# A diffusion layer with expert retrieval: last heads of two blocks ahead of the late projections, PSUM banks used twice, and modulation rows by a transpose and DRAM

## Chip, cores and metric

One core of one Trainium2 chip runs the whole program. TensorE (PE) does the matmuls, VectorE (DVE), ScalarE (ACT) and GpSimd (POOL) the rest, SyncE (SP) issues most of the DMAs. The metric is the device time of one execution in microseconds; less is better. The kernel before took 1765.1 us (median of 3 runs, 1762.88 to 1768.2).

## The reference

One layer on 512 latent tokens of 1024 features (with 256 context tokens that only the scans read), all in float32. What matters of it:

```
m = silu(c) @ w_ada + b_ada                       # 6 * 1024 values
sh1, sc1, g1, sh2, sc2, g2 = split(m, 6)
u   = (layer_norm(x) * (1 + sc1) + sh1) @ w_in
mix = two_way_scans(u)                            # 8 heads of 128, RMS norm and gates
x   = layer_norm(ALPHA * x + g1 * (mix @ w_out), ln_gamma[0], ln_beta[0])
h   = layer_norm(x) * (1 + sc2) + sh2
y   = peer(h)        # queries, top 16 of 128 x 128 keys, 8 heads, gathered experts
x   = layer_norm(ALPHA * x + g2 * y, ln_gamma[1], ln_beta[1])
```

The four rows g1, sh2, sc2 and g2 have 1024 values each, one for each feature, and are wanted on all 128 partitions, since tokens lie on partitions.

## The kernel before

The program goes through the stages scans (`mixer`, to about 434 us), output projection with its norms (`out_proj_early` and `out_proj`, to about 496 us), retrieval (`Peer.run`, to about 1724 us) and a tail with the last norm (`finish`). A scheduler sets the order of instructions on each engine by priorities and data, except in stretches that are marked as ordered by hand; ACT in the tail is one (its order is that of the code).

**Modulation.** `mods_second` multiplies 24 columns of 128 weights with silu(c) on DVE (`column`, L215) and gathers the sums as columns of the tile `m2` [128, 32]: columns 0 to 7 are g1, 8 to 15 sh2, 16 to 23 sc2, 24 to 31 g2 (those by `mods_last` during the retrieval). To turn eight columns into a row on all partitions, `mod_half` (L259) lets PE multiply each column, broadcast to 128 x 128, with the identity, four to a bank of 512 (`prow`, L265; the trace counts two instructions for each), and ACT copies the bank (L267). g1 is then multiplied into w_out on DVE (L232), half by half. `mod_row` (L269) does both halves of a row, for sc2 at the end of `out_proj_early`, sh2 in `out_proj`, and g2 in the tail.

**Output projection.** Tokens form four blocks of 128. Seven of eight heads are ready early: blocks 0 and 1 (`NB` = 2) are projected during the scans and kept as `parts` together with ALPHA times x (L662). When the last head is there (`lasth`, `lastl`: high and low part of float32 in the fast matmul type, so each product is three matmuls, L139 to L141), the loop over b (L719 to L755) does for each block: a matmul with the identity that brings `parts` into PSUM (b < 2, L725), the last head's three matmuls for each half, statistics on DVE (L727), the norm's affine steps (`affine`, L134 and L135) into x1, a second norm and its affine into h2 with sc2 and sh2, eight transposes on PE (`pht`, L749) and the split into hh (ACT, L751) and hl (DVE, L752). Blocks 2 and 3 are projected inside the loop by `late_block` (L704), after block 0 and after block 1: ALPHA x by a matmul (L709, tile `xe`), then 42 matmuls of seven heads. Accumulators are the banks `po` (blocks 0 and 1, one after the other), `pl2` (block 2) and `pl3` (block 3), two banks each; `pht` has the other two. After the last head of block 3 come the first queries of blocks 0 and 1 (`first_queries(0)`, 48 matmuls, into `po`) and their scores (`pss`, L764), which share the loop's end with the norm of block 3; `first_queries(2)` closes the stage.

**Tail.** `rows` (a tile `Gn`) holds g2, ln_gamma and ln_beta. `finish` (L1187) is called for block 3 (its y is `yg` in SBUF) and blocks 0 to 2: y times g2 (L1195), plus ALPHA x1 (L1196), statistics (L1197), affine (L134, L135) and a write to the output (L1201). PE still combines y of blocks 0 to 2 while this runs.

Of the kernel before, what the change touches and what calls it, by code (L numbers as in the profile page):

```python
# [19 lines left out]
D = 1024  # L20
# [11 lines left out]
class Net:  # L32
# [155 lines left out]
    def mods_second(self, pers, pool):  # L188

        nc, a = self.nc, self.a
        H = D // 2
        mm = pool.tile([128, 24, 2], F32, name="m2h")
        self.m2 = pers.tile([128, 32], F32, name="m2")
        self.b2 = pers.tile([128, 32], F32, name="b2col")
        nc.sync.dma_start(self.b2, a["b2col"])
        nc.vector.tensor_scalar(self.b2[:, 16:24], self.b2[:, 16:24], 1.0, None, op0=OP.add)
        gain = pool.tile([128, 2], F32, name="gain")
        nc.sync.dma_start(gain, a["gains"])  # L200
        sr = pool.tile([128, 2, H], F32, name="silrow")
        for h in range(2):
            cr, t1 = (pool.tile([128, H], F32, name="wada2", bufs=3) for _ in range(2))
            nc.sync.dma_start(cr, a["crow"][:, h * H:(h + 1) * H].to_broadcast([128, H]))
            self.log_sigmoid(sr[:, h], cr, t1, t1)
            nc.scalar.activation(sr[:, h], sr[:, h], AF.Exp)
            nc.vector.tensor_tensor(sr[:, h], sr[:, h], cr, op=OP.mult)
        nc.sync.dma_start(self.sild, sr[0:1].rearrange("p h k -> p (h k)"))
        yield True

        def column(j):
            for h in range(2):
                w = pool.tile([128, H], F32, name="wada2", bufs=3)
                nc.sync.dma_start(w, a["w_ada2"][j, h])
                nc.vector.scalar_tensor_tensor(w, w, 1.0, sr[:, h], op0=OP.mult, op1=OP.mult,  # L215
                                               accum_out=mm[:, j, h:h + 1])

        def close(js):
            nc.vector.tensor_tensor(self.m2[:, js], mm[:, js, 0], mm[:, js, 1], op=OP.add)
            nc.vector.tensor_tensor(self.m2[:, js], self.m2[:, js], self.b2[:, js], op=OP.add)  # L220
        for j in range(8):
            column(j)
            if j % 2:
                yield True
        close(slice(0, 8))
        for hf in range(2):
            g1 = pool.tile([128, H], F32, name="g1")
            self.mod_half(g1, self.pj, 0, hf, "pj")
            for k in range(8):
                raw = pool.tile([128, H], F32, name="wada2", bufs=3)  # L230
                nc.sync.dma_start(raw, a["w_out"][k * 128:(k + 1) * 128, hf * H:(hf + 1) * H])
                nc.vector.scalar_tensor_tensor(raw, raw, gain[:, k // 4:k // 4 + 1], g1, op0=OP.mult, op1=OP.mult)  # L232
                hi = pool.tile([128, H], F32R, name="wosh")
                nc.scalar.activation(hi, raw, AF.Copy)
                nc.vector.tensor_tensor(raw.bitcast(F32R), raw, hi, op=OP.subtract)
                for i, t in enumerate((hi.bitcast(F32), raw)):
                    nc.sync.dma_start(self.wod[hf, i, :, k, :], t)
                yield True
                if k % 2:
                    j = 8 + hf * 8 + k - 1  # L240
                    column(j)
                    column(j + 1)
                    yield True
        close(slice(8, 24))

    def mods_last(self, pool):

# [8 lines left out]
            yield  # L256
        nc.vector.tensor_tensor(m2, m2, self.b2[:, 24:32], op=OP.add)

    def mod_half(self, out, ps, i, hf, ptag):  # L259

        nc = self.nc
        p = ps.tile([128, 512], F32, name="prow", tag=ptag)
        for k in range(4):
            j = i * 8 + hf * 4 + k
            nc.tensor.matmul(p[:, k * 128:(k + 1) * 128], self.m2[:, j:j + 1].to_broadcast([128, 128]),  # L265
                             self.ident, start=True, stop=True)
        nc.scalar.activation(out, p, AF.Copy)  # L267

    def mod_row(self, pool, ps, i, name, ptag):  # L269
        r = pool.tile([128, D], F32, name=name)  # L270
        for hf in range(2):
            self.mod_half(r[:, hf * 512:(hf + 1) * 512], ps, i, hf, ptag)
        return r


    def first_norm(self, pool, ps, xt, b):
# [361 lines left out]
    def out_proj_early(self, last, ps):  # L638
# [11 lines left out]
        for b in range(NB):  # L650
# [8 lines left out]
            for hf in range(2):  # L659
# [1 line left out]
                x, p = (t.rearrange("p (k c) -> p k c", k=4) for t in (xs[hf], ps_[hf]))  # L661
                nc.vector.scalar_tensor_tensor(r, x, ALPHA, p, op0=OP.mult, op1=OP.add)  # L662
                self.parts[b, hf] = r
        self.sc2 = self.mod_row(wo, ps, 2, "sc2", "pj2")

    def out_proj(self, pool, mpool, pers, ps, last):
        nc, a = self.nc, self.a
# [17 lines left out]
        nc.sync.dma_start(bet, a["ln_b"][0:1].to_broadcast([128, D]))  # L685
        self.sk = pers.tile([128, 2, 128], F32, name="sk")
        nc.sync.dma_start(self.sk, a["skT"])
        sh2 = self.mod_row(pool, ps, 1, "sh2", "pht")
        slabs, self.q0 = [], []
        for i in range(2):  # L690
            qh, ql = (mpool.tile([128, 8, 128], F32R, name=f"{n}{i}") for n in ("wq0h", "wq0l"))
# [6 lines left out]
        nc.vector.tensor_scalar(aid, self.ident, ALPHA, None, op0=OP.mult)  # L698

        banks = lambda n: [ps.tile([128, 512], F32, name=f"{n}{hf}", bufs=1) for hf in range(2)]  # L700
        r3, r0, r2 = (banks(n) for n in ("pl3", "po", "pl2"))
        rl = {0: r0, 2: r2, 3: r3}

        def late_block(b):  # L704
            sl = slice(b * 128, (b + 1) * 128)
# [4 lines left out]
            for g in self.groups:  # L710
                self.project_heads(rl[b], g, self.split_heads(g, sl), False, False)

        def first_queries(b0):
            cs = slice(b0 * 128, (b0 + 2) * 128)
            for (qh, ql), p, q in zip(slabs, banks("po"), self.q0):
                for k in range(8):
                    self.mm3(p[:, cs], qh[:, k, :], ql[:, k, :], self.hh[:, k, cs], self.hl[:, k, cs], k == 0, k == 7)
                nc.scalar.activation(q[:, cs], p[:, cs], AF.Copy)
        for b in range(4):  # L719
            sl = slice(b * 128, (b + 1) * 128)  # L720
            st = pool.tile([128, 2, 6], F32, name="sto", bufs=2)
            r = rl[b] if b in rl else banks("po")
            for hf, (wh, wl) in enumerate(self.w):
                if b < NB:
                    nc.tensor.matmul(r[hf], self.ident, self.parts[b, hf], start=True, stop=False)  # L725
                self.mm3(r[hf], lh[:, sl], ll[:, sl], wh[:, last, :], wl[:, last, :], False, True)
                nc.vector.bn_stats(st[:, hf, :], r[hf])  # L727
            if b == 3:
                first_queries(0)
                self.yg = pers.tile([128, D], F32, name="yg")  # L730
                self.S0 = self.yg.rearrange("p (b s n) -> p b s n", b=4, s=2)
                self.scores(self.q0, ps, "pht", [((0, 2), lambda s: self.S0[:, 0:2, s, :])])
            x1 = x1s[b] if b < 2 else pool.tile([128, D], F32, name="x1", bufs=2)
            stats = self.norm_scale(pool, st, "o")
            for hf, p in enumerate(r):
                cs = slice(hf * 512, (hf + 1) * 512)
                self.affine(x1[:, cs], p, stats, gam[:, cs], bet[:, cs])
            nc.scalar.dma_start(self.x1d[b], x1)
            h2 = (h2s[b] if b < 2 else pers.tile([128, D], F32, name="h2_3") if b == 3 else
                  pool.tile([128, D], F32, name="h2", bufs=2))  # L740
            stats = self.norm_stats(pool, x1, "p")
            for cs in (slice(0, 512), slice(512, D)) if b == 3 else (slice(0, D),):
                self.affine(h2[:, cs], x1[:, cs], stats, sc2[:, cs], sh2[:, cs])
            self.h2[b] = h2
            for g in range(2):
                p = ps.tile([128, 4, 128], F32, name="pht")
                for k in range(4):
                    kk = g * 4 + k
                    nc.tensor.transpose(p[:, k, :], h2[:, kk * 128:(kk + 1) * 128], self.ident)  # L749
                hi, lo = self.hh[:, g * 4:g * 4 + 4, sl], self.hl[:, g * 4:g * 4 + 4, sl]  # L750
                nc.scalar.activation(hi, p, AF.Copy)  # L751
                nc.vector.tensor_tensor(lo, p, hi, op=OP.subtract)  # L752
            if b < NB:
                late_block(b + NB)
        first_queries(2)  # L755

    def scores(self, qT, ps, tag, dst):

# [143 lines left out]
class Peer:  # L902
# [300 lines left out]
    def run(self, es, out):  # L1203
# [14 lines left out]
        with ExitStack() as e0:  # L1218
# [78 lines left out]
            with ExitStack() as e1:  # L1297
# [38 lines left out]

                rows = w.tile([128, NG, self.GN, self.GT], F32, name="Gn", bufs=2)
                rows = rows.rearrange("p g n t -> p (g n t)").rearrange("p (i d) -> p i d", i=3)
                for hf in range(2):
                    n.mod_half(rows[:, 0, hf * 512:(hf + 1) * 512], hps, 3, hf, "pH")  # L1340
                nc.sync.dma_start(rows[:, 1], a["ln_g"][1:2].to_broadcast([128, D]))
                nc.sync.dma_start(rows[:, 2], a["ln_b"][1:2].to_broadcast([128, D]))
                nc.scalar.preload_act_table_set("natural_log_exp_and_others")
# [9 lines left out]
def build(tc, a, out):  # L1353
    with ExitStack() as es:
        n = Net(tc, a)
        n.h2 = {}
        n.consts(es)
        dp = es.enter_context(tc.tile_pool(name="x1d", bufs=1, space=bass.MemoryType.DRAM))
        n.x1d = dp.tile([4, 128, D], F32, name="x1d")
        n.wod = dp.tile([2, 2, 128, 8, 512], F32, name="wod")  # L1360
        n.sild = dp.tile([1, D], F32, name="sild")
        n.mixer(es)
        Peer(n).run(es, out)

# [16 lines left out]
```

## Time and profile before

| what | us or share |
|---|---|
| median of 3 runs (lowest, highest) | 1765.1 (1762.88, 1768.2) |
| the profiled execution's own time | 1758.76 |
| its span | 1756.6 |
| PE busy | 1699.8, 97% |
| weight loads (PEld) | 1486.9, 85% |
| DVE busy | 1447.2, 82% |
| ACT busy | 833.2, 47% |
| POOL busy | 406.7, 23% |

The span is what the trace shows between the first and the last instruction; 2.2 us of the execution lie around it. All rows below are from this one execution. A row of a timeline is a group of instructions that follow each other; its bracket says how long the engine stood idle before it and what ended that. Matmuls overlap, so that the start of the next row says more than the length of the last.

### The profile page before, as it was taken

Reading aid. Unit: us, or ns where it says so; the run is one execution under the profiler, and the core shown is the slowest. Engines: PE = TensorE matmul, PEld = TensorE weight load, DVE = VectorE, ACT = ScalarE, POOL = GpSimd, SP = SyncE. Lnnn points to the kernel's source line nnn. Section 1 sums busy time; section 2 is a strip of 40 time slices with the busy share of each in tenths; the row PEclk is TensorE's granted clock in tenths of the full one; section 3 lists DMA queues with packets and bytes.
Section 4 is the critical chain, followed back from the end, with each engine's and each line's share of the span. In section 5 each row is a group of like instructions: output and inputs, shape, how many; then the busy total and the mean of one; then the engine's idle time right before and its main releaser. Section 6 shows DMA issues by size and latency. Waiting matters only on the chain. (4 is left out here: it accounts for less than half of the span.)

```text
span 1756.6 us, 28197 instructions
## 1 busy us (share of the span) xinstructions
PE 1699.8 (97%) x10501; PEld 1486.9 (85%) x10501; DVE 1447.2 (82%) x2917; ACT 833.2 (47%) x1417; POOL 406.7 (23%) x286
## 2 busy tenths in 40 slices
PE   6999999989999999999999999999999999999997
PEld 3888877877778999999998999999999998888886
DVE  6688988877779999999996878777777786776768
ACT  4677677655133355676674333333333333333332
POOL 0000000000023102238422544443444342111000
PEclk8999999999989999999999999999999999999999
DMA  8444435242322257989999999989999989999862
GB/s 321 122 127 162 139 96 182 95 179 101 108 73 85 73 152 290 332 298 322 332 333 355 368 341 351 323 304 334 325 309 338 321 299 309 351 332 305 270 217 96
DMA packets 174811, 428.99 MB, mean 244 GB/s; under 512 B 14993, under 2 KB 78801, under 8 KB 170578
## 3 DMA queue, kind: packets, MB, share of 16 engines
q1 hardware_dynamic: 137234, 290.87, 48.5%
q0 software_dynamic: 36864, 134.23, 21.8%
q8 instruction: 82, 1.34, 0.3%
q10 hardware_dynamic: 576, 2.10, 0.3%
q14 instruction: 55, 0.45, 0.1%
HBM read 378.38 MB, written 48.76 MB: 243 GB/s over the span
## 5 line engine op out<-in xcount | busy, mean ns | idle before, releaser
L139 PE MATMUL pH<-hh,uh 128*128 128x384 f32 x1024 | 350.3, 342 | 1.1 <-ACT gels L1111 1.1
L141 PE MATMUL pH<-hh,ul 128*128 128x384 f32 x1024 | 347.7, 340 | 1.5 <-DVE ul L1098 1.5
L140 PE MATMUL pH<-hl,uh 128*128 128x384 f32 x1024 | 347.0, 339 | 0.0
L139 PE MATMUL y<-vh,ah 128*128 128x512 f32 x768 | 302.8, 395 | 2.9 <-ACT ah L1137 2.9
L140 PE MATMUL y<-vl,ah 128*128 128x512 f32 x768 | 301.5, 393 | 0.1
L141 PE MATMUL y<-vh,al 128*128 128x512 f32 x768 | 301.5, 394 | 0.0
L1098 DVE TENSOR_TENSOR vl<-vr,vh 128x1024 fp32r<-128x1024 f32 x128 | 156.7, 1224 | 151.7 <-ACT vh L1096 150.7
L1167 POOL DMA_INDIRECT erow<-in_u_dram,ix x128 | 187.8, 1467 | 370.4 <-DVE scr L1176 219.1
L1167 POOL DMA_INDIRECT erow<-in_v_dram,ix x128 | 185.4, 1448 | 327.3 <-DVE yg L1184 179.8
L1096 ACT ACTIVATE vh<-vr 128x1024 fp32r<-128x1024 f32 x128 | 135.1, 1057 | 195.2 <-issue 125.9
L1137 ACT ACTIVATE ah<-gel 128x384 fp32r<-128x384 f32 x128 | 66.8, 524 | 276.6 <-DVE gel L1134 273.6
L139 PEld LDWEIGHTS pH<-hh,uh 128*128 128x128 f32 x1024 | 192.4, 188 | 3.8 <-ACT gels L1111 1.4
L140 PEld LDWEIGHTS pH<-hl,uh 128*128 128x128 f32 x1024 | 192.8, 188 | 2.7
L141 PEld LDWEIGHTS pH<-hh,ul 128*128 128x128 f32 x1024 | 192.4, 188 | 2.6 <-DVE ul L1098 2.4
L1096 ACT ACTIVATE uh<-ur 128x1024 fp32r<-128x1024 f32 x128 | 135.0, 1056 | 121.2 <-PE pH L140 75.3
L141 PEld LDWEIGHTS y<-vh,al 128*128 128x128 f32 x768 | 144.9, 189 | 33.6
L139 PEld LDWEIGHTS y<-vh,ah 128*128 128x128 f32 x768 | 144.7, 188 | 33.0 <-ACT ah L1137 3.4
L140 PEld LDWEIGHTS y<-vl,ah 128*128 128x128 f32 x768 | 144.9, 189 | 30.6 <-DVE vl L1098 0.5
L1098 DVE TENSOR_TENSOR ul<-ur,uh 128x1024 fp32r<-128x1024 f32 x128 | 155.6, 1216 | 16.0 <-PE pH L141 13.9
L1184 DVE SCALAR_TENSOR_TENSOR yg<-erow,act,yg 128x1024 f32<-128x1024 f32 x127 | 162.2, 1277 | 0.1
L1176 DVE SCALAR_TENSOR_TENSOR scr<-erow,h 128x1024 bf16<-128x1024 f32 x128 | 155.8, 1218 | 0.0
L139 PE MATMUL pc<-hTh,wh 128*128 128x512 f32 (+1 forms) x304 | 109.5, 360 | 0.9 <-ACT V L407 0.7
(367 smaller groups left out, 3047.0 us busy)
## 6 DMA issues: line engine op xcount, KB each, us to landing
ur<-in_uT_dram SPq DMA_DIRECT2D x128, 512.0 KB
vr<-in_v_dram SPq DMA_DIRECT2D x128, 512.0 KB
Gd<-stage SPq DMA_DIRECT2D x24, 1024.0 KB
Gn<-Gd SPq DMA_DIRECT2D x16, 1536.0 KB
wraw<-in_w_cf_dram SPq DMA_DIRECT2D x24, 512.0 KB
wada<-in_w_ada_dram SPq DMA_DIRECT2D x48, 256.0 KB
Hd<-gels SPq DMA_DIRECT2D x56, 192.0 KB
gel<-Hd SPq DMA_DIRECT2D x56, 192.0 KB
```

The lines of the kernel that those rows point to most:

```text
L139: mm(out, lh, rh, start=start, stop=False)
L140: mm(out, lh, rl, start=False, stop=False)
L141: mm(out, ll, rh, start=False, stop=stop)
L1096: nc.scalar.activation(hi, raw, AF.Copy)
L1098: sub = eng.tensor_tensor(lo, raw, hi, op=OP.subtract)
L1137: nc.scalar.activation(ah, g, AF.Copy)
L1167: nc.gpsimd.indirect_dma_start(out=e, out_offset=None, in_=a[src], in_offset=bass.IndirectOffsetOnAxis(ap=self.ix[:, j:j + 1], axis=0))
L1176: nc.vector.scalar_tensor_tensor(scr, e, 1.0, h2, op0=OP.mult, op1=OP.mult, accum_out=dots[:, j:j + 1])
L1184: nc.vector.scalar_tensor_tensor(y, e, act[:, j:j + 1], y, op0=OP.mult, op1=OP.add)
```

## The change

**Rows.** `mod_half` goes. `to_rows` takes n columns of `m2` (8 or 16), transposes them with one PE instruction into [n, 128], copies that with ACT and writes it to a DRAM tile `m2d` from GpSimd's queue. The new `mod_row` reads a row back from `m2d` to all partitions, from GpSimd's queue too. g1 is written as a row once and read in two halves, sh2 and sc2 are written together at the end of `mods_second`, g2 in the tail. The columns 8 and 9 of `mods_second` move ahead of the work on w_out.

**Order.** The loop's body becomes two functions, `last_head(b)` and `norms(b)`, and the calls are written out. The banks are `po`, `pl1` and `pl2` for blocks 0, 1 and 2, and `po` once more for block 3; the first queries go into `pl1` (blocks 0 and 1) and `pl2` (blocks 2 and 3).

```diff
-            self.mod_half(g1, self.pj, 0, hf, "pj")
+            self.mod_row(g1, 0, slice(hf * H, (hf + 1) * H))
...
+    def to_rows(self, js, pool, ps, tag):
+
+        nc, n = self.nc, js.stop - js.start
+        p = ps.tile([n, 128], F32, name="prow", tag=tag)
+        nc.tensor.transpose(p, self.m2[:, js], self.ident)
+        r = pool.tile([24, 128], F32, name="mrows")[0:n]
+        nc.scalar.activation(r, p, AF.Copy)
+        nc.gpsimd.dma_start(self.m2d[0, js, :], r)
+
+    def mod_row(self, out, i, cs=slice(0, D)):
+
+        row = self.m2d[:, i * 8:(i + 1) * 8, :].rearrange("o j p -> o (j p)")[:, cs]
+        self.nc.gpsimd.dma_start(out, row.to_broadcast([128, cs.stop - cs.start]))
...
-        self.sc2 = self.mod_row(wo, ps, 2, "sc2", "pj2")
+        self.sc2 = wo.tile([128, D], F32, name="sc2")
+        self.mod_row(self.sc2, 2)
...
-        r3, r0, r2 = (banks(n) for n in ("pl3", "po", "pl2"))
-        rl = {0: r0, 2: r2, 3: r3}
+        rl = [banks(n) for n in ("po", "pl1", "pl2")]
+        sts = [pool.tile([128, 2, 6], F32, name="sto", bufs=4) for _ in range(4)]
...
+        last_head(0)
+        last_head(1)
+        norms(0)
+        late_block(2)
+        last_head(2)
+        norms(1)
+        rl.append(banks("po"))
+        late_block(3)
+        last_head(3)
+        norms(2)
+        first_queries(0, (0, 1))
+        self.yg = pers.tile([128, D], F32, name="yg")
+        self.S0 = self.yg.rearrange("p (b s n) -> p b s n", b=4, s=2)
+        self.scores(self.q0, ps, "pht", [((0, 2), lambda s: self.S0[:, 0:2, s, :])])
+        norms(3)
+        first_queries(2, (0, 1))
...
-                for hf in range(2):
-                    n.mod_half(rows[:, 0, hf * 512:(hf + 1) * 512], hps, 3, hf, "pH")
+                n.to_rows(slice(24, 32), w, hps, "pH")
+                n.mod_row(rows[:, 0], 3)
```

How this moves instructions, at the places where it matters. PE before, from the last projection of the scans' stage (`pe`) to late block 2 (`pl_4800`):

```order
L141 MATMUL pe<-wo_4593,mTl 128x512
L265 MATMUL prow<-ident,m_985 128x128 x13
L725 MATMUL po_4798<-part,ident 128x512
L139 MATMUL po_4798<-wo_4591,lasth 128x512
L140 MATMUL po_4798<-wo_4592,lasth 128x512
L141 MATMUL po_4798<-wo_4591,lastl 128x512
L725 MATMUL po_4799<-mT,ident 128x512
L139 MATMUL po_4799<-wo_4593,lasth 128x512
L140 MATMUL po_4799<-wo_4594,lasth 128x512
L141 MATMUL po_4799<-wo_4593,lastl 128x512
L709 MATMUL pl_4800<-xe,aident 128x512
```

PE in the changed kernel, the second part of the same place (block 0's last head ends in `po_4776`, block 1's is `pl_4777` and `pl_4778`, late block 2 begins with `xe`):

```order
L141 MATMUL po_4776<-wo_4594,lastl 128x512
L722 MATMUL pl_4777<-part,ident 128x512
L139 MATMUL pl_4777<-wo_4592,lasth 128x512
L140 MATMUL pl_4777<-wo_4593,lasth 128x512
L141 MATMUL pl_4777<-wo_4592,lastl 128x512
L722 MATMUL pl_4778<-mT,ident 128x512
L139 MATMUL pl_4778<-wo_4594,lasth 128x512
L140 MATMUL pl_4778<-wo_4595,lasth 128x512
L141 MATMUL pl_4778<-wo_4594,lastl 128x512
L714 MATMUL pl_4779<-xe,aident 128x512
```

The 13 matmuls for rows are gone, and block 1's last head stands ahead of late block 2. DVE in the changed kernel, from the statistics of block 0 (`po_4775`, `po_4776`; x_4753 and h_4747 are its x1 and h2) on, with block 1 (`pl_4777`, `pl_4778`, x_4754) between:

```order
L134 SCALAR_TENSOR_TENSOR x_4753<-po_4775,mvo,gam_4755 128x512
L724 BN_STATS sto<-pl_4777 128x6
L135 SCALAR_TENSOR_TENSOR x_4753<-x_4753,rso,bet_4757 128x512
L724 BN_STATS sto<-pl_4778 128x6
L134 SCALAR_TENSOR_TENSOR x_4753<-po_4776,mvo,gam_4755 128x512
L119 BN_STATS stp<-x_4753 128x6
L135 SCALAR_TENSOR_TENSOR x_4753<-x_4753,rso,bet_4757 128x512
L125 BN_AGGR mvo<-sto 128x2
L119 BN_STATS stp<-x_4753 128x6
L134 SCALAR_TENSOR_TENSOR x_4754<-pl_4777,mvo,gam_4755 128x512
L125 BN_AGGR mvp<-stp 128x2
L134 SCALAR_TENSOR_TENSOR x_4754<-pl_4778,mvo,gam_4755 128x512
```

Before, block 0's steps stood alone there. DVE before, the last two blocks (`pl_4800` is block 2, `pl_4796` and `pl_4797` block 3):

```order
L727 BN_STATS sto<-pl_4800 128x6
L727 BN_STATS sto<-pl_4801 128x6
L727 BN_STATS sto<-pl_4796 128x6
L125 BN_AGGR mvo<-sto 128x2
L727 BN_STATS sto<-pl_4797 128x6
L134 SCALAR_TENSOR_TENSOR x_5015<-pl_4800,mvo,gam_4765 128x512
```

In the changed kernel the statistics of block 3 (`po_4937`, `po_4938`) stand behind all steps of block 2. The tail: ACT before, and then ACT in the changed kernel:

```order
L1096 ACTIVATE vh<-vr 128x1024
L1137 ACTIVATE ah<-gel 128x384
L267 ACTIVATE Gn<-prow 128x512 x2
L1343 ACT_TABLE_LOAD
L127 ACTIVATE rsz<-mvz,eps 128x1
```

```order
L1112 ACTIVATE vh<-vr 128x1024
L1153 ACTIVATE ah<-gel 128x384
L270 ACTIVATE mrows<-prow 8x128
L1359 ACT_TABLE_LOAD
L127 ACTIVATE rsz<-mvz,eps 128x1
```

ACT's copy stands in the same place; behind it GpSimd's order now ends with a write of mrows to m2d (L271) and a read of m2d to Gn (L276), the latter waiting for the former.

## Rows read from the trace of the kernel before

**Rows 1.** Windows: from:to, us, busy (count) by engine, PE clock, DMA share, GB/s.

```profile
475.00:500.00 25.00, 17.44 (x100) 15.18 (x98) 14.07 (x22) 10.95 (x22) 1.03 (x3) 0.73 0.26 95
500.00:525.00 25.00, 25.00 (x121) 20.73 (x121) 25.00 (x159) 7.28 (x11) 9.79 (x5) 1.00 0.36 106
900.00:1400.00 500.00, 497.15 (x2610) 454.70 (x2609) 397.17 (x503) 185.99 (x278) 211.73 (x162) 1.00 0.95 333
```

**Rows 2.** Timeline of PE, 434 to 499: start, us, engine, line, operation, tile [idle before].

```profile
434.25 3.06 PE L265 MATMUL prow<-ident,m 128*128 128x128 f32 x26
437.15 1.02 PE L725 MATMUL po<-part,ident 128*128 128x512 f32 x2
...
440.26 1.88 PE L709 MATMUL pl<-xe,aident 128*128 128x512 f32 x4
...
452.56 1.02 PE L725 MATMUL po<-part,ident 128*128 128x512 f32 x2
...
463.87 1.06 PE L749 MATMUL pht<-ident,h 128*128 128x128 f32 x8
...
467.99 0.40 PE L139 MATMUL pl<-wo,lasth 128*128 128x512 f32 x1
...
470.78 0.28 PE L139 MATMUL po<-hh,wq0h 128*128 128x256 f32 x1
...
479.60 1.94 PE L749 MATMUL pht<-ident,h 128*128 128x128 f32 x8 [3.20 <-DVE h L135]
482.10 2.08 PE L764 MATMUL pss<-sk,q 128*128 128x128 f32 x8 [0.56 <-DVE hl L752]
486.70 1.97 PE L749 MATMUL pht<-ident,h 128*128 128x128 f32 x8 [2.52 <-DVE h L135]
488.50 0.79 PE L139 MATMUL po<-hh,wq0h 128*128 128x256 f32 x2
...
495.96 1.35 PE L764 MATMUL pss<-sk,q 128*128 128x128 f32 x8
...
498.73 0.50 PE L139 MATMUL pq<-hh,wqh 128*128 128x512 f32 x1 [0.71 <-ACT wqh L943]
```

**Rows 3.** Timeline of DVE, 438 to 488.

```profile
438.90 0.70 DVE L727 BATCH_NORM_STATS2 sto<-po 128x6 f32<-128x512 f32 x1
...
447.31 1.28 DVE L135 SCALAR_TENSOR_TENSOR h<-h,rsp,sh 128x1024 f32<-128x1024 f32 x1
...
468.89 2.10 DVE L727 BATCH_NORM_STATS2 sto<-pl 128x6 f32<-128x512 f32 x3 [2.45 <-PE pl L141]
...
485.89 1.41 DVE L135 SCALAR_TENSOR_TENSOR h<-h,rsp,sh 128x512 f32<-128x512 f32 x2
```

**Rows 4.** Timeline of SP near 470: the first loads of the retrieval.

```profile
470.05 1.73 SPq L1093 DMA_DIRECT2D ur<-in_uT_dram  x3
```

**Rows 5.** Timelines of ACT and DVE in the tail.

```profile
1725.42 1.06 ACT L267 ACTIVATE Gn<-prow 128x512 f32<-128x512 f32 x2
```

```profile
1726.75 1.28 DVE L1195 TENSOR_TENSOR vr<-yg,Gn 128x512 f32<-128x512 f32 x2
...
1751.89 1.41 DVE L135 SCALAR_TENSOR_TENSOR vr<-vr,rsz,Gn 128x512 f32<-128x512 f32 x2
```

**Rows 6.** Timelines of several engines: issues of DMAs and the first steps behind them.

```profile
0.74 0.39 SPq L785 DMA_DIRECT2D cc<-in_ccol_dram  x1
...
1.19 1.84 SPq L280 DMA_DIRECT2D xin<-in_x_dram  x4
...
2.43 0.22 ACT L109 ACTIVATE cct<-cc 128x16 f32<-128x16 f32 x1 [0.41 <-DMA cc<-in_ccol_dram]
...
4.87 0.69 DVE L119 BATCH_NORM_STATS2 sta<-xin 128x6 f32<-128x512 f32 x1 [0.97 <-DMA xin<-in_x_dram]
...
1648.36 1.01 POOL L1167 DMA_INDIRECT erow<-in_v_dram,ix  x1 [7.10 <-DVE yg L1184]
```

**Rows 7.** Timeline of DVE in the scans: the first use of g1.

```profile
131.83 0.75 DVE L232 SCALAR_TENSOR_TENSOR wada<-wada,gain,g 128x512 f32<-128x512 f32 x1 [0.39 <-ACT g L267]
```

More of the change, by code (lines that the diff above doesn't have):

```diff
@@ L225, in mods_second @@
         close(slice(0, 8))
+        self.to_rows(slice(0, 8), pool, self.pj, "pj")
+        column(8)
+        column(9)
+        yield True
         for hf in range(2):
             g1 = pool.tile([128, H], F32, name="g1")
-            self.mod_half(g1, self.pj, 0, hf, "pj")
+            self.mod_row(g1, 0, slice(hf * H, (hf + 1) * H))
             for k in range(8):
@@ L238, in mods_second @@
                 yield True
-                if k % 2:
-                    j = 8 + hf * 8 + k - 1
+                j = 10 + hf * 8 + k - 1
+                if k % 2 and j < 24:
                     column(j)
@@ L244, in mods_second @@
         close(slice(8, 24))
+        self.to_rows(slice(8, 24), pool, self.pj, "pj")
     def mods_last(self, pool):
@@ L257, in mods_last @@
         nc.vector.tensor_tensor(m2, m2, self.b2[:, 24:32], op=OP.add)
[L259 to L270, printed above, removed]
-        for hf in range(2):
-            self.mod_half(r[:, hf * 512:(hf + 1) * 512], ps, i, hf, ptag)
-        return r
+    def to_rows(self, js, pool, ps, tag):
[8 more added lines that the diff above has]
+        self.nc.gpsimd.dma_start(out, row.to_broadcast([128, cs.stop - cs.start]))
     def first_norm(self, pool, ps, xt, b):
@@ L687, in out_proj @@
         nc.sync.dma_start(self.sk, a["skT"])
-        sh2 = self.mod_row(pool, ps, 1, "sh2", "pht")
+        sh2 = pool.tile([128, D], F32, name="sh2")
+        self.mod_row(sh2, 1)
         slabs, self.q0 = [], []
@@ L711, in late_block, with last_head, norms @@
                 self.project_heads(rl[b], g, self.split_heads(g, sl), False, False)
[L713 to L719, printed above, removed]
+        def last_head(b):
             sl = slice(b * 128, (b + 1) * 128)
-            st = pool.tile([128, 2, 6], F32, name="sto", bufs=2)
-            r = rl[b] if b in rl else banks("po")
             for hf, (wh, wl) in enumerate(self.w):
                 if b < NB:
[L725 to L732, printed above, removed]
+                    nc.tensor.matmul(rl[b][hf], self.ident, self.parts[b, hf], start=True, stop=False)
+                self.mm3(rl[b][hf], lh[:, sl], ll[:, sl], wh[:, last, :], wl[:, last, :], False, True)
+                nc.vector.bn_stats(sts[b][:, hf, :], rl[b][hf])
+        def norms(b):
+            sl = slice(b * 128, (b + 1) * 128)
             x1 = x1s[b] if b < 2 else pool.tile([128, D], F32, name="x1", bufs=2)
-            stats = self.norm_scale(pool, st, "o")
-            for hf, p in enumerate(r):
+            stats = self.norm_scale(pool, sts[b], "o")
+            for hf, p in enumerate(rl[b]):
                 cs = slice(hf * 512, (hf + 1) * 512)
@@ L752, in out_proj, with first_queries @@
                 nc.vector.tensor_tensor(lo, p, hi, op=OP.subtract)
-            if b < NB:
-                late_block(b + NB)
-        first_queries(2)
+        def first_queries(b0, js):
+            cs = slice(b0 * 128, (b0 + 2) * 128)
+            for j, p in zip(js, banks(("pl1", "pl2")[js[0] // 2])):
+                qh, ql = slabs[j]
+                for k in range(8):
+                    self.mm3(p[:, cs], qh[:, k, :], ql[:, k, :], self.hh[:, k, cs], self.hl[:, k, cs], k == 0, k == 7)
+                nc.scalar.activation(self.q0[j][:, cs], p[:, cs], AF.Copy)
+        last_head(0)
[14 more added lines that the diff above has]
+        first_queries(2, (0, 1))
     def scores(self, qT, ps, tag, dst):
@@ L1338, in run @@
                 rows = rows.rearrange("p g n t -> p (g n t)").rearrange("p (i d) -> p i d", i=3)
-                for hf in range(2):
-                    n.mod_half(rows[:, 0, hf * 512:(hf + 1) * 512], hps, 3, hf, "pH")
+                n.to_rows(slice(24, 32), w, hps, "pH")
+                n.mod_row(rows[:, 0], 3)
                 nc.sync.dma_start(rows[:, 1], a["ln_g"][1:2].to_broadcast([128, D]))
@@ L1361, in build @@
         n.sild = dp.tile([1, D], F32, name="sild")
+        n.m2d = dp.tile([1, 32, 128], F32, name="m2d")
         n.mixer(es)
```

## The prediction

> **What bounds the kernel now.** I read the page's engine shares first, where TensorE (PE) is far ahead. The table by windows then shows where it is not busy: from 500 us on it is full (25.00 of 25, then 497.15 of 500 us between 900 and 1400), while 475 to 500 us has 17.44 busy us of 25 and a mean granted clock of 0.73 [rows 1]. So a microsecond taken from PE's path near 480 us should shift all that follows, up to the last stage. PE's timeline around that window [rows 2] shows three things: 26 L265 matmuls (the modulation rows) between the last projection and the first L725; three idle spells of 3.20, 0.56 and 2.52 us, two of them ended by DVE's h; and matmuls at the lower clock level after the first of them (8 transposes in 1.94 us instead of 1.06). DVE's timeline shows why [rows 3]: blocks 0 and 1 are normed at leisure, but the statistics of blocks 2 and 3 start together at 468.89, and DVE needs until 487.3 (485.89 + 1.41) for both. Last I read the end [rows 5]: from 1726.75 DVE alone, without a gap, sets it; it waits for nothing of PE by then, and its last step runs to 1753.3.
>
> **The change, late projections (gain).** Durations are from [rows 2].
> - Rows off PE: 434.25 to 437.15 falls away, 2.90 us. Everything else that the first last head reads is there by then. Six more prow matmuls go from the scans' end; at the same 0.112 us each that is 0.7, which I count at nothing and keep as a bound.
> - New order: four half heads of blocks 0 and 1 take 2 x 3.11 = 6.2 us (437.15 to 440.26 is two), so late block 2 starts at 434.25 + 6.2 = 440.45. Its transposes of h 0 now stand after the xe matmuls (1.3 us, the 1.88 of the row at 440.26 less its overlap) and 30 more of 0.23 us: PE is there at 448.7. DVE's chain for h 0 takes 9.7 us from its first statistics in the old trace (438.90 to 447.31 + 1.28, [rows 3]). Now 3.4 us of steps of block 1 and 1.2 of wq0l stand between; it can start 1.9 us sooner, and the old chain's gaps, some 1.6 us in all, are filled: 448.6 + 4.6 - 1.9 - 1.6 = 449.7, a wait of 1.0 us. Bounds: 0 (block 1's steps fill DVE's gaps) and 2.5 (block 1 wholly ahead). h 1 is ready before its transposes.
> - Two late blocks of 12.3 us (440.26 to 452.56 is one, with 8 transposes) and four half heads without the identity matmul (467.99 to 470.78: 2.8 us) follow, so head 3 ends at 440.45 + 1.0 + 24.6 + 2.8 = 468.9, against 470.78: 1.9 us gained.
> - Norm 2 now starts after head 2, at about 455, and has all of late block 3 (12 us) to run beside: 9.7 us fit. Norm 3 alone remains. After 468.9 PE has the transposes of h 2 (1.06), the first queries of blocks 0 and 1 (5.5, from 470.78 on) and the scores (1.06 at the full level): until 476.5. Norm 3 from 468.2 takes 9.7, less the last half affine: first half of h 3 at 477.6. PE idles 1.1 us where it idled 6.28. Then transposes to the first query 1.6 and 48 matmuls 5.5: end 484.7.
> - Before, the same point was 495.96. The gain is 11.2 us: 1.9 up to head 3, 5.2 of idle time, and 4.1 of clock (1.94 + 2.08 + 1.80 + 7.46 = 13.3 us at the lower level, 9.2 at the full one).
>
> The clock is the weak term. The row at 498.73 shows 0.71 us of idle time with no loss of level behind it, the one at 479.60 shows 3.20 with a loss; 1.1 us lies between, nearer to the first, so I take no loss. With a loss, h 3's transposes and some 17 of the 48 queries take 2.9 us more. Bounds of the gain: 11.2 - 2.9 - 1.5 = 6.8 and 11.2 + 1.0 + 0.7 = 12.9.
>
> What is late next: ACT's and DVE's first work for the retrieval follows the same queries, and the window 500 to 525 has PE and DVE both at 25.00 [rows 1]; both start earlier by the same amount. The first retrieval rows (ur) are issued at 470.05 [rows 4], as a buffer comes free; at 3.7 us for 512 KB [rows 6] they are there by about 476, and ACT would want them at about 478. So the gain should carry.
>
> **The second and third rows (sh2, sc2).** They now come by GpSimd's queue: a transpose, an ACT copy, one write, two reads, all after the L215 columns that end long before. sc's read waits for DVE's L662, which reads the tile that it overwrites and follows PE's last projection (before 434.25), so by the 3.7 us of [rows 6] and an issue it lands at about 440. Its first reader is the step of h 0 just ahead of the old row at 447.31 [rows 3], about 446: six microseconds of cover, and past them every further one would be added to the wait for h 0. On GpSimd only casts and wql of the retrieval stand behind it.
>
> **g1 in the scans.** Both halves are now read back from DRAM. In the old trace the first half came from ACT and DVE waited 0.39 us for it [rows 7]; now it comes 6 to 8 us later (the round trip priced below), at 137.5 to 139.5, and its first reader stands later in DVE's order too, among steps that the old trace has at 139 to 140 us. The second half is needed 40 us after its issue. PE loses 32 small matmuls there beside other work. I take 0, from -1.5 (PE's share of them on the path) to +3 (the row late, the queue of scan steps behind it on DVE).
>
> **The tail (loss).** The row g2 was 16 matmuls and two ACT copies, ready just as DVE began (1725.42 + 1.06 against 1726.75, [rows 5]). Now ACT's copy of 8x128 stands in the same place, behind the last ah, and ends at about 1725.7. Then GpSimd writes 4 KB to DRAM, waits for it, and reads 512 KB back. The first DVE step that needs it (vr from yg and Gn) has the whole finish of four blocks behind it on DVE, 26.5 us without a gap, so all of the delay shows at the end. No row has such a round trip. Nearest rows [rows 6]: 8 KB issued at 0.74 let ACT start at 2.43, 1.7 us; 512 KB issued at 1.19 let DVE start at 4.87, 3.7 us; one GpSimd issue takes 1.01 us. Low end: 1725.7 + 1.7 + 3.7 = 1731.1, a loss of 4.4. High end: for a write the only price is the last output block, 3.3 us from DVE's last step (1753.3) to the end of the span (1756.6), 1.6 more than the 1.7; with it and an issue of 1.0 in front of either transfer 1734.7, a loss of 8.0. Below zero is excluded, since both transfers start after 1725.7. The xin rows are from a start with many loads at once, and the tail is quiet, so I take 5.4, near the low end.
>
> The trace thus makes the two transfers 5.4 to 9.0 us. The Trainium skill, "DMA: Bandwidth & Descriptors", section "Anatomy of one DMA — SWDGE (gpsimd) path", gives a fit of about 2.0 us plus bytes by 436 GB/s for a transfer from this queue, most of the fixed part being the receipt of the write. By that page the estimate is 2.0 + 3.2 = 5.2 us, a loss of 4.2 at the end and a sum 1.2 us better; so it speaks against this edit too, only less. No row here shows what the queue takes for such a copy.
>
> **Sum.** -11.2 + 0 + 5.4 = -5.8 us. Against the profiled execution's own 1758.76 that is 1753.0. That execution was 6.3 us faster than the median of the shown runs; applied to the median, 1765.1 - 5.8 = 1759.3.
>
> **Rivals.**
> 1. *The gain stays in part.* PE falls to the lower level once more after waiting for h 3, or waits longer for h 0: gain 6.8 to 8.5, net -1.4 to -3 with the tail: 1762 to 1764, no measurable change. For it: the wait of 1.1 us is still there. Against: 0.71 us cost nothing.
> 2. *The round trip is cheap and the gain full.* Tail at its low end, +4.4, gain 12 to 12.9: net -7.6 to -8.5, 1756.6 to 1757.5. For it: the quiet tail. Against: the 1.01 us issues.
> 3. *Slower: the gain is eaten on the way and the tail is not.* From 500 us on the transfers would have to set the pace: the DMA share is 0.95 from 900 to 1400 [rows 1]. If PE runs into loads that don't come sooner, it gives back what it gained, and the row's wait of 5.4 to 8.0 us stands: 1770.5 to 1773.1. It ends above the time before once under half of the 11.2 us reaches the tail (5.4 of 11.2), and measurably above once nothing does, or under a quarter where the wait is 8.0. Against it: PE's idle time in those 500 us is only 2.85 us in all, and a load is issued when a buffer comes free, which PE and DVE decide.
> 4. *The first g1 half is late*, with DVE held for up to 3 us in the scans: 1762.3.
> 5. *The change does not do what it says*: norm 2 does not run beside late block 3, since its steps queue on DVE behind block 1. Then PE idles as before and only 2 us are won; with the tail 1768 to 1769. The order of DVE's steps speaks against it.
>
> **Numbers.** Forecast as worked out: 0.42, with its own range 1757 to 1762. Rivals: 1 has 0.20, 2 has 0.18, 3 has 0.08, 4 has 0.07, 5 has 0.05. A measurement of this kernel can tell about 0.3%, 5.3 us, from no change: faster means under 1759.8, slower over 1770.4. The forecast lies just at the first bound, so its 0.42 splits into 0.28 faster and 0.14 same; rival 2 is faster, and 1, 4 and 5 are mostly same (0.04 of them faster); rival 3 is slower, with 0.02 more from 5 with a dear tail. Faster 0.50, same 0.40, slower 0.10. The range leaves out rival 3 and the dear end of 5, and takes in rival 2 with PE's part of g1: 1756.6 - 1.5, and another 1.6 for the 0.3 us by which each of five terms may be off: 1753.5 to 1768.
>
> **What would show it.** the last scores (L764, the row at 495.96) at 484 to 486, with one idle spell before h 3 and none before h 2; a full granted clock from 475 to 500; DVE's first finish step 4 to 8 us after its last al, waiting for a DMA; no new idle time on DVE near 140. Wrong would be: lower clock again after the wait for h 3, PE idle before the transposes of h 0 by over 2.5 us, or a finish that starts without a wait.

## The result

The changed kernel took 1754.46 us (median of 17 runs, 1749.8 to 1762.33), the kernel before on the same chips 1765.68 us (17 runs, 1759.6 to 1773.25). The ratio is 0.994, with a 95% interval from 0.9927 to 0.9953: a gain of 0.5 to 0.7%, beyond the 0.3% that a measurement can tell. Measured again later, with 12 runs beside 33, it was 0.9957 (0.9935 to 0.9978). The measured time lies in the stated range (1753.5 to 1768), 1.0 us inside its lower end, but below the 1757 to 1762 that the forecast had for itself: it said 5.8 us less, and the two measurements have 10.6 and 7.6 us less. Its steps are held against the traces below.

The profile of the changed kernel has a span of 1750.9 us against 1756.6. First the page's engine shares and the windows that answer to [rows 1]; columns as there.

```profile
PE 1692.9 (97%) x10440; PEld 1477.1 (84%) x10440; DVE 1446.2 (83%) x2917; ACT 829.9 (47%) x1412; POOL 416.6 (24%) x294
```

```profile
475.00:500.00 25.00, 22.43 (x133) 18.67 (x131) 16.78 (x85) 10.48 (x18) 5.62 (x4) 1.00 0.30 101
900.00:1400.00 500.00, 497.44 (x2573) 454.21 (x2571) 393.95 (x499) 183.97 (x267) 213.67 (x163) 1.00 0.95 334
```

The window that had 17.44 busy us at a granted clock of 0.73 has 22.43 at 1.00, and its end is already retrieval. PE's timeline of the changed kernel, the rows that answer to [rows 2]:

```profile
435.11 0.39 PE L141 MATMUL pe<-wo,mTl 128*128 128x512 f32 x1
435.33 1.02 PE L722 MATMUL po<-part,ident 128*128 128x512 f32 x2
...
441.52 1.88 PE L714 MATMUL pl<-xe,aident 128*128 128x512 f32 x4
...
450.50 1.09 PE L744 MATMUL pht<-ident,h 128*128 128x128 f32 x8 [0.26 <-DVE h L135]
...
469.18 1.03 PE L744 MATMUL pht<-ident,h 128*128 128x128 f32 x8
...
475.71 1.35 PE L780 MATMUL pss<-sk,q 128*128 128x128 f32 x8
478.02 1.38 PE L744 MATMUL pht<-ident,h 128*128 128x128 f32 x8 [0.96 <-DVE h L135]
...
485.41 1.35 PE L780 MATMUL pss<-sk,q 128*128 128x128 f32 x8
...
488.18 0.50 PE L139 MATMUL pq<-hh,wqh 128*128 128x512 f32 x1 [0.71 <-ACT wqh L959]
```

Here h 0 to h 3 stand for h2 of the blocks 0 to 3, and the second scores are those of blocks 2 and 3. The last head starts 0.22 us behind the last projection, h 0 is waited for 0.26 us, h 2 not at all, h 3 0.96 us, and the second scores stand at 485.41 instead of 495.96. In the kernel before, the last projection is the row below, 3.13 us ahead of the first last head at 437.15:

```profile
434.02 0.39 PE L141 MATMUL pe<-wo,mTl 128*128 128x512 f32 x1
```

Why h 2 is not waited for shows on DVE. In the changed kernel the statistics of block 2 and the last step of its norm are these; late block 3 stands on PE from 455.60 to 467.55:

```profile
455.32 1.29 DVE L724 BATCH_NORM_STATS2 sto<-pl 128x6 f32<-128x512 f32 x2
...
465.55 1.28 DVE L135 SCALAR_TENSOR_TENSOR h<-h,rsp,sh 128x1024 f32<-128x1024 f32 x1
```

In the tail, `al` is the low part of the retrieval's activations; its last one is the last step of the retrieval on DVE. DVE, GpSimd and ACT, answering to [rows 5]:

```profile
1716.08 0.55 DVE L1154 TENSOR_TENSOR al<-gel,ah 128x384 fp32r<-128x384 f32 x1
1721.97 1.29 DVE L1211 TENSOR_TENSOR vr<-yg,Gn 128x512 f32<-128x512 f32 x2 [5.33 <-DMA Gn<-m2d]
...
1746.20 1.41 DVE L135 SCALAR_TENSOR_TENSOR vr<-vr,rsz,Gn 128x512 f32<-128x512 f32 x2
```

```profile
1715.77 0.58 POOL L271 DMA_DIRECT2D m2d<-mrows  x1 [76.93 <-ACT mrows L270]
1718.32 0.57 POOL L276 DMA_DIRECT2D Gn<-m2d  x1 [1.97 <-DMA m2d<-mrows]
```

```profile
1715.22 0.25 ACT L270 ACTIVATE mrows<-prow 8x128 f32<-8x128 f32 x1
```

DVE stands idle for 5.33 us after its last al, until the row is back from DRAM. From the start of that last al to the start of the last affine row it is 30.12 us. Before, it is 25.61, from the row below to 1751.89 [rows 5]:

```profile
1726.28 0.55 DVE L1138 TENSOR_TENSOR al<-gel,ah 128x384 fp32r<-128x384 f32 x1
```

### The profile page after: what moved, and what is told of

It reads as the page before. It is cut to its first block, busy times and chain, and to the rows that moved or that the text cites. A ratio compares the mean times of both kernels' runs of the same rounds, so it can differ in the third digit from the quotient of the medians.

```text
span 1750.9 us, 28102 instructions
## 1 busy us (share of the span) xinstructions
PE 1692.9 (97%) x10440; PEld 1477.1 (84%) x10440; DVE 1446.2 (83%) x2917; ACT 829.9 (47%) x1412; POOL 416.6 (24%) x294
```

## Experiments

To compare stages whatever came ahead of them, I take three stretches from each trace. The **stage** runs from the start of the first last head to the first query matmul of the retrieval (437.15 and 498.73 before). The **retrieval** runs from there to the start of DVE's last al, the **tail** from there to the start of the last affine row.

| kernel | start of first last head | stage | retrieval | tail |
|---|---|---|---|---|
| before | 437.15 | 61.6 | 1227.6 | 25.6 |
| before, again | 440.22 | 61.6 | 1231.1 | 25.6 |
| changed | 435.33 | 52.9 | 1227.9 | 30.1 |
| changed, again | 435.17 | 53.0 | 1236.8 | 30.5 |
| order alone | 438.43 | 52.6 | 1232.6 | 25.6 |
| rows alone | 434.56 | 61.2 | 1241.0 | 30.5 |
| filled waits | 438.63 | 59.0 | 1236.4 | 25.6 |
| head of block 2 early alone | 438.61 | 55.4 | 1238.5 | 25.6 |
| heads of 0 and 1 early alone | 440.23 | 61.6 | 1231.9 | 25.6 |
| g2 by SP | 433.08 | 53.0 | 1237.3 | 28.7 |
| g2 on PE | 435.43 | 53.0 | 1233.6 | 25.6 |
| g2 early | 435.48 | 52.8 | 1235.8 | 23.2 |
| g2 early, again | 435.58 | 53.0 | 1236.3 | 23.2 |

Among kernels with the same order or the same tail, stage and tail repeat within 0.4 us. The retrieval scatters over 13 us for the same work. The start scatters over 7, but not at random: the six executions with the rows on PE have 437.15 to 440.23 (mean 438.9), the seven with the rows through DRAM 433.08 to 435.58 (mean 434.9). Of these 4.0 us, 2.9 are the row matmuls ahead of the first last head; the scans ahead of them end about 1.0 us sooner as well, which is not clear of its scatter (0.6 us).

**The kernel before, again** (no edit).

> The kernel before once more, for a second trace of it. The profiled execution shown (1758.76 us) lies 6.9 us under the median of 17 runs of the same kernel (1765.68), while that of the changed kernel (1752.71) lies 1.8 under its own. Theory A (scatter): the ratio is 1.000, within 0.2%, the out-projection stage again ends with the scores at 496 us within 1.5, and what a longer execution has more lies elsewhere. Rival B (the stage itself is longer in most executions, and the change gains more there than the one trace let see): the scores stand at 499 to 502.

Measured: ratio 1.0021 (0.9999 to 1.0044), span 1763.2. The stage is the same row for row:

```profile
482.67 1.94 PE L749 MATMUL pht<-ident,h 128*128 128x128 f32 x8 [3.20 <-DVE h L135]
485.17 2.07 PE L764 MATMUL pss<-sk,q 128*128 128x128 f32 x8 [0.56 <-DVE hl L752]
489.76 1.97 PE L749 MATMUL pht<-ident,h 128*128 128x128 f32 x8 [2.52 <-DVE h L135]
499.05 1.34 PE L764 MATMUL pss<-sk,q 128*128 128x128 f32 x8
```

The scores stand at 499.05, a place that I had given to rival B, but not for its reason: the idle times are those of [rows 2] to the hundredth, and all is 3.1 us later because the scans ended later. The other 3.5 us are in the retrieval. So theory A on the stage; single executions differ by what lies around it.

**Order alone.** Into the kernel before, only the new calls and banks; rows on PE.

```diff
-        r3, r0, r2 = (banks(n) for n in ("pl3", "po", "pl2"))
+        rl = [banks(n) for n in ("po", "pl1", "pl2")]
...
+        last_head(0)
+        last_head(1)
+        norms(0)
+        late_block(2)
+        last_head(2)
+        norms(1)
...
```

> Only the new order and the banks; the modulation rows by PE as before. Theory A (the sum of the prediction): all of the 11.2 us but the 2.9 of the row matmuls, and no wait in the tail: -8.3 us, a ratio of 0.9953, and the second scores at 487.7. Rival B (the five more microseconds in the medians belong to the order): -13, 0.9926. Rival C (most of the gain was the row matmuls, PE waits for the norms as before): -2 to -4, 0.998.

Measured: ratio 0.9965 (0.9944 to 0.9986), -6.2 us with an interval from -9.9 to -2.5. That holds theory A's -8.3 and leaves out B's -13; C's -2 to -4 is not left out by the time, but by the stage, which is 9.0 us shorter and has 0.96 us of waiting for h in place of 5.72. The second scores are at 488.22.

**Rows alone.** The changed kernel with the old loop over b.

```diff
-        rl = [banks(n) for n in ("po", "pl1", "pl2")]
+        r3, r0, r2 = (banks(n) for n in ("pl3", "po", "pl2"))
+        rl = {0: r0, 2: r2, 3: r3}
...
-        last_head(0)
-        last_head(1)
-        norms(0)
...
+        for b in range(4):
```

> Only the rows by a transpose and DRAM; the order of the late projections as before. Theory A: 2.9 us less on PE ahead of the first last head, which carries to the end, against 5.4 in the tail: +2.5 us, a ratio of 1.0014, and the first finish step on DVE 5.4 us behind the last al. Rival B (the rows give the further five microseconds, in the scans or later): -2.5, 0.9986. Rival C (norms 2 and 3 wait for DVE anyway and the 2.9 us are lost in that wait): +5.4, 1.0031.

Measured: ratio 1.0009 (0.9988 to 1.0031), between A and no change. C's 1.0031 is the end of this interval, so it falls by the trace: the 2.9 us ahead of the first last head are gone and are not waited away, since the stage behind them is 61.2 us (61.6 before). The tail shows the same gap:

```profile
1736.75 0.55 DVE L1143 TENSOR_TENSOR al<-gel,ah 128x384 fp32r<-128x384 f32 x1
1743.04 1.29 DVE L1200 TENSOR_TENSOR vr<-yg,Gn 128x512 f32<-128x512 f32 x2 [5.74 <-DMA Gn<-m2d]
```

-2.9 on PE, -0.4 in the stage and +4.9 in the tail make +1.6 us, a ratio of 1.0009. This half of the change, on its own, gains nothing.

**The changed kernel, again** (no edit).

> The changed kernel once more, on the chip of these runs. By the traces so far the stage up to the first retrieval queries is 11.6 us shorter and the tail 4.5 longer: -7.1 us, a ratio of 0.9960. Theory A (that account is whole, and the -0.60% measured first has scatter of the retrieval in it): 0.995 to 0.997, stage and tail within 0.5 us of the first trace. Rival B (something else is won as well, some 3.5 us): 0.994 again.

Measured: 0.9957 (0.9935 to 0.9978), with stage and tail within 0.4 us of the first trace. The account by stages (below) gives 0.9960.

**Two pieces of the order.** Both cuts of the edit are shown against *order alone*; the rows are on PE. First the last head of block 2 ahead of late block 3, with that of block 1 still behind late block 2.

```diff
         last_head(0)
-        last_head(1)
         norms(0)
         late_block(2)
+        last_head(1)
         last_head(2)
```

> The kernel before with one piece of the order: the last head of block 2 ahead of late block 3 (and with it block 3 in the banks of block 0); the last head of block 1 stays behind late block 2, the rows stay on PE. From the first last head to the first retrieval queries the kernel before takes 61.6 us, the whole new order 52.6. Theory A (the gain of 9.0 is norm 2 running beside late block 3, and the last heads of blocks 0 and 1 add nothing of their own): 52.5 to 54.5. Rival B (norms 1 and 2 then collide on DVE and the heads of blocks 0 and 1 must go first): 56 to 59.

Measured: a stage of 55.4 us, between the two theories; ratio 0.9972 (0.9945 to 0.9998). PE waits for h 2 no more, but 2.88 us for h 3, and the granted clock of the window is 0.93:

```profile
475.28 1.03 PE L739 MATMUL pht<-ident,h 128*128 128x128 f32 x8
478.54 1.35 PE L775 MATMUL pss<-sk,q 128*128 128x128 f32 x8
482.76 1.84 PE L739 MATMUL pht<-ident,h 128*128 128x128 f32 x8 [2.88 <-DVE h L135]
```

```profile
475.00:500.00 25.00, 20.73 (x132) 18.29 (x131) 15.57 (x50) 10.96 (x21) 3.22 (x3) 0.93 0.39 127
```

On DVE, norms 1 and 2 now run side by side: norm 2 ends 36.2 us after the first last head, against 31.5 in the changed kernel.

Then the other piece: the last heads of blocks 0 and 1 first, that of block 2 behind late block 3.

```diff
         late_block(2)
-        last_head(2)
         norms(1)
         rl.append(banks("po"))
         late_block(3)
+        last_head(2)
         last_head(3)
```

> The other piece: the last heads of blocks 0 and 1 ahead of late block 2, but the last head of block 2 behind late block 3, together with that of block 3; rows on PE. Theory A: norms 2 and 3 start together again, PE idles over 5 us and the granted clock of the stage's last 25 us is 0.7 to 0.8; 61 to 62 us from the first last head to the first retrieval queries, as before. Rival B: 56 to 59.

Measured, by one execution: a stage of 61.6 us, as before, with PE idle for 3.01, 0.56 and 2.52 us and this window:

```profile
475.00:500.00 25.00, 18.88 (x117) 17.35 (x116) 15.68 (x25) 9.04 (x20) 0.69 (x2) 0.73 0.40 141
```

Theory A. This kernel has the new banks too, so the banks alone bring nothing. The two pieces don't add: one alone is worth 6.2 us, the other nothing, both 9.0. Block 1's head ahead of late block 2 takes norm 1 out of the way of norm 2; without norm 2 in that place there is nothing to take it out of the way of.

**Filled waits.** The kernel before with 50 matmuls that nothing reads, in PE's waits.

```diff
-                first_queries(0)
+                spare = first_queries(0)
+                fill(spare, 28, slabs[0][0][:, 0, :])
...
+                fill(spare, 22, self.hh[:, 7, 256:384])
```

> The kernel before, with 50 more matmuls of 256 columns whose results nothing reads: 28 behind the first queries of blocks 0 and 1, 22 around and behind their scores, so that PE is busy while it waits for the norms of blocks 2 and 3. Theory A (the lower granted clock comes from those waits and costs up to 4.1 us): the granted clock of 475 to 500 us stays near 1.00, the 8 transposes take 1.06 instead of 1.94, the last 48 queries 5.5 instead of 7.46, and the stage ends 2.5 to 4 us sooner though PE does more; a ratio of 0.998. Rival B (the clock falls whatever PE does there, or the norms on DVE set the end alone): the stage ends within 0.7 us of before, or later.

Measured: the stage takes 59.0 us instead of 61.6, with PE's window at the full level; 0.9997 (0.9972 to 1.0022) in time, which can't tell 2.6 us.

```profile
475.00:500.00 25.00, 22.09 (x167) 19.63 (x166) 16.55 (x32) 11.23 (x23) 2.11 (x3) 1.00 0.35 120
```

```profile
478.35 2.77 PE L723 MATMUL po<-hh,wq0h 128*128 128x256 f32 x22 [0.47 <-ACT q L718]
481.08 1.07 PE L756 MATMUL pht<-ident,h 128*128 128x128 f32 x8
...
487.47 1.38 PE L756 MATMUL pht<-ident,h 128*128 128x128 f32 x8 [0.80 <-DVE h L135]
```

The 8 transposes take 1.07 us (1.94 in [rows 2]) though PE does more work in all: theory A on the clock. In this stage the lower level goes with PE's waits, and it costs 2.6 us on the path. The rest of the gain comes from when DVE has h 3: its transposes start 49.55 us after the first last head before, 48.84 with the waits filled and 42.69 in the changed kernel, and from there to the first query matmul of the retrieval it is 12.03, 10.17 and 10.16 us.

**g2 through SP's queue.**

```diff
-        self.nc.gpsimd.dma_start(out, row.to_broadcast([128, cs.stop - cs.start]))
+        (q or self.nc.gpsimd).dma_start(out, row.to_broadcast([128, cs.stop - cs.start]))
...
+                n.to_rows(slice(24, 32), w, hps, "pH", nc.sync)
+                n.mod_row(rows[:, 0], 3, q=nc.sync)
```

> The changed kernel, but in the tail the write of the row g2 and its read are issued by SP instead of GpSimd; place and data are the same. Theory A (what costs is the round trip through DRAM, twice the time of a transfer): the first finish step again stands 4.5 to 6 us behind the last al, within 0.7 us of the 5.4 of the changed kernel. Rival B (GpSimd's queue is what makes it dear): 3.5 us or less. Rival C (SP has loads and waits of its own in front): over 7.

Measured: DVE waits 3.89 us between the end of its last al and its first finish step; ratio 0.9944 (0.9918 to 0.997). That lies between A's 4.5 to 6 and B's 3.5: neither theory as written. SP's issues, then DVE's step:

```profile
1722.79 0.29 SPq L271 DMA_DIRECT2D m2d<-mrows  x1
1724.02 0.33 SPq L276 DMA_DIRECT2D Gn<-m2d  x1
```

```profile
1727.82 1.29 DVE L1211 TENSOR_TENSOR vr<-yg,Gn 128x512 f32<-128x512 f32 x2 [3.89 <-DMA Gn<-m2d]
```

From the write's issue to the read's it is 1.23 us (2.55 on GpSimd), from there to DVE 3.80. On GpSimd the read takes 3.65 in the first trace of the changed kernel and 4.06 and 4.05 in its second and in *rows alone*, so the two queues don't differ clearly in the read; the write and the wait for it are dearer by 1.3 us on GpSimd's. So most of the delay is the round trip, about a quarter of it the queue, by one trace on SP against three.

**g2 on PE.**

```diff
-                n.to_rows(slice(24, 32), w, hps, "pH")
-                n.mod_row(rows[:, 0], 3)
+                for hf in range(2):
+                    n.mod_half(rows[:, 0, hf * 512:(hf + 1) * 512], hps, 3, hf, "pH")
```

> The changed kernel, but the row g2 in the tail by 16 matmuls and two ACT copies as before; the other rows and the order stay changed. Theory A: no wait in the tail, the finish takes the 25.6 us from the last al of before; with the 11.6 of the stage -11.6 us, a ratio of 0.9934, 4.5 less than the changed kernel. Rival B (the finish is as late by PE's 16 matmuls, the wait merely moves): no difference to the changed kernel within 1 us.

Measured: 0.9941 (0.9919 to 0.9963), with no wait in the tail:

```profile
1722.00 0.55 DVE L1164 TENSOR_TENSOR al<-gel,ah 128x384 fp32r<-128x384 f32 x1
1722.47 1.29 DVE L1221 TENSOR_TENSOR vr<-yg,Gn 128x512 f32<-128x512 f32 x2
```

The tail is 25.6 us again (1747.62 less 1722.00), so the trace bears out theory A; the interval reaches from -14.3 to -6.5 us and includes the changed kernel's own.

**g2 early.** Transpose and copy where the columns are done, the write ahead of the tail; only the read stays in the tail's code.

```diff
+        yield
+        yield
+        self.g2row = self.to_rows(slice(24, 32), w, ps, "pH", False)
...
+                nc.gpsimd.dma_start(n.m2d[0, slice(24, 32), :], n.g2row)
...
-                n.to_rows(slice(24, 32), w, hps, "pH")
```

> The changed kernel, but the row g2 is transposed and copied when its columns are summed (two steps of the loop later), written to DRAM ahead of the tail, and read back by GpSimd as the tail begins. Theory A (the round trip alone makes the gap of 5.4 us in the tail): DVE starts the finish behind its last al without a gap, 5.4 us less than the changed kernel, and against the kernel before 0.9907 by the two traces (-11.1 and the 5.4: -16.5 by the medians). Rival B (another thing sets the end of the tail as soon as the row is there, PE's last y or the ln rows): only 0 to 2 us less than the changed kernel, 0.993 to 0.994.

> The changed kernel with the row g2 written and read ahead of the tail, once more, for a closer interval. By the traces: 11.6 us from the stage and 2.4 from the tail, where half of the first finish now runs ahead of the last al: -14.0 us, a ratio of 0.9921 (Theory A). Rival B (the stage gains only and the tail gives nothing): 0.9935 or more.

Measured: 0.9914 (0.9885 to 0.9943), and again 0.992 (0.9892 to 0.9948): -15 and -14 us, against -10.6 and -7.6 of the changed kernel. GpSimd and DVE in the first of the two traces:

```profile
1647.19 0.58 POOL L1349 DMA_DIRECT2D m2d<-mrows  x1
1696.21 0.58 POOL L281 DMA_DIRECT2D Gn<-m2d  x1 [48.44 <-DMA gel<-Hd]
```

```profile
1717.32 0.69 DVE L1216 TENSOR_TENSOR vr<-yg,Gn 128x512 f32<-128x512 f32 x1
...
1724.13 0.55 DVE L1159 TENSOR_TENSOR al<-gel,ah 128x384 fp32r<-128x384 f32 x1
1724.60 0.69 DVE L1218 BATCH_NORM_STATS2 stz<-vr 128x6 f32<-128x512 f32 x1
```

The two intervals don't quite leave out rival B's 0.9935, but the tail does: it is 6.9 us shorter than in the first trace of the changed kernel. That is more than theory A's 5.4, which had the finish start behind the last al. The read, issued in the first trace 21 us ahead of its first use, is there in time for DVE to do five steps of the first finish in gaps ahead of its last al, so that the tail is 2.4 us shorter than before instead of 4.5 longer. Its ratios are the lowest of the versions tried, though their intervals overlap that of g2 on PE.

## Why the prediction was right, point by point

- *Rows off PE, 2.90 us.* Right: the gap between the last projection and the first last head went from 3.13 to 0.22 us.
- *h 0, a wait of 1.0 us (0 to 2.5).* 0.26 us. Counted from the first last head, DVE had h 0 after 15.1 us where I had 15.4, and PE came to it some 0.4 us later than I had it; with the rows still on PE (order alone) there is no wait at all.
- *Norm 2 beside late block 3.* Right: its statistics start at 455.32 (I had about 455), and there is no wait for h 2. That it takes both pieces of the order was in no step: I had called only the place of the last head of block 2 a reason, and alone that leaves 2.88 us of waiting for h 3.
- *Idle 1.1 us, no loss of clock behind it.* 0.96 us, and the window's clock is 1.00. The weak term held.
- *Stage, 11.2 us.* 2.91 of rows and 61.6 - 52.9 = 8.7 behind them: 11.6 us. The total is near, but its split was off, and the errors cancel: I had 5.2 of idle time and 4.1 of clock, and the filled waits show 2.6 for the clock. I had counted the slow matmuls one by one, but those ahead of h 3 mostly ran inside the wait for DVE and hid there: at the full level h 3's transposes start only 0.7 us sooner, and what follows them takes 1.9 us less. The part that comes from DVE's norms is larger by about as much.
- *It carries.* Right, but two traces don't show it: from the first query matmul to the last al the first trace of each kernel takes 1227.6 and 1227.9 us, in a stretch that scatters by 13. What shows it are the times: order alone -6.2 us (-9.9 to -2.5) for 9.0 in the stage, g2 on PE -10.4 (-14.3 to -6.5) for 11.6, g2 early -15 and -14 for 14.0. So the gain arrives in the main; a loss of a few microseconds on the way can't be excluded.
- *sh2, sc2 and g1 at nothing.* sc2's read was issued at 436.52 and no step waited for it. The loss that I allowed for in the scans didn't come; if anything they end about 1.0 us sooner (the starts above), inside my bound of 1.5. The first half of g1 was written at 131.74 and read back at 133.73, and its first reader on DVE, later in the order as assumed, does not wait (compare [rows 7]):

```profile
141.22 0.75 DVE L236 SCALAR_TENSOR_TENSOR wada<-wada,gain,g 128x512 f32<-128x512 f32 x1
```

- *Tail, 5.4 us (4.4 to 8.0).* The wait was 5.33 and 5.74. That it fits so well is partly luck: the rows' sum gave 4.4, and the 1.0 us that I put on top had no term of its own. One term that I had not: the finish itself took 24.2 instead of 25.1 us from its first step to its last. DVE did equal steps in pairs there, probably because y of the next block was ready by then. So the loss at the end was 4.5 to 4.9. The parts were 2.55 for the write up to the read's issue and 3.65 to 4.06 for the read, against the 1.7 and 3.7 of [rows 6]; the write was short. The Trainium skill ("DMA: Bandwidth & Descriptors", "Anatomy of one DMA — SWDGE (gpsimd) path") gave an estimate of 2.0 + 3.2 = 5.2 us for both. The traces have 6.2 to 6.6, so this estimate is short on the write and on the read.
- *Sum, -5.8 us.* The account of the traces is -2.9 - 8.7 + 4.5 = -7.1, a ratio of 0.9960, and the two profiled executions differ by 5.7 in their spans. The first measurement, 0.994, lies 3.5 us beyond the account and its interval ends 1.2 us short of it; the second, 0.9957, agrees. The 1.0 us by which the scans may end sooner are not in the account; with them it is -8.1, just short of the -8.3 at which the first interval ends. So -5.8 was too small by the tail's finish (0.5 to 0.9), the stage (0.4) and perhaps the scans. What the first measurement had beyond that is not settled. The retrieval scatters by 13 us for equal work: in the second trace of the changed kernel PE has 194.77 busy us of 200 between 700 and 900 (199.39 in the first) and DVE waits 6.2 us for one gathered row. Whether the change shifts that by a microsecond or two I can't tell from these runs.

Of the rivals, the partial gain fell with the clock that stayed. The second was half right: the round trip is not cheap (6.2 us), but the loss of 4.5 at the end and the gain of 11.6 are near its 4.4 and 12, and the account of -7.1 lies nearer to its -7.6 than to -5.8. The eaten gain fell with the times; the late g1 with the row above; and that norm 2 would queue behind block 1 is half there: it is what the new place of block 1's head prevents.

## What to carry to other kernels

Where a matmul engine waits for a chain on another engine, ask which accumulators could be finished earlier, and then whether that other engine is free at that time: here the early head of block 2 needed block 1's norm out of the way first. A row through DRAM was a good trade in the middle of this program, where no step waited for it, and a bad one at the point where the last stage did; write such a row as soon as its values exist. Compare single stages across traces when single executions scatter by more than the edit is worth.

## What the runs showed of the hardware

- Waits of PE of 0.71, 0.80 and 0.96 us in this stage left the granted clock of the window at 1.00 (the level of 2.4 GHz); with one wait of 2.88 us it was 0.93, and with waits of 3.20, 0.56 and 2.52 us 0.73. The 8 transposes behind the waits of 2.88 and 3.20 took 1.84 and 1.94 us, against 1.03 to 1.07 without a wait. With the longer waits filled by matmuls that nothing reads it was 1.00.
- The 4 KB write to DRAM and the wait for it cost 2.55 us on GpSimd's queue (three traces) and 1.23 on SP's (one); the 512 KB read back took 3.65 to 4.06 and 3.80 from its issue to the first step that used it.
- Equal work in the retrieval took 1227.6 to 1241.0 us from one execution to the next.
